# Keys and values of two heads in seven products instead of eight, and half of the gate-stage logits summed on ScalarE

## The chip, the cores and the metric

The kernel runs on one core of a Trainium2 chip. The metric is the device time of one execution in microseconds (us). TensorE (PE in the profile) multiplies matrices, VectorE (DVE) and ScalarE (ACT) work elementwise, GpSimd (POOL) and SyncE (SP) here mostly start transfers.

## What is computed

One decoder layer of a model with two branches side by side, for 528 prompt rows (16 of them meta tokens) and 32 sample rows (8 sequences of 4), so 560 rows in all, of width 2048.

```python
h = rmsnorm(x, g_pre)
q, k, v, ga, cb, cc, ch, gc, ma, mc = jnp.split(h @ w_in, split_offsets(), axis=-1)
a = attend(q, k, v, b_sb).reshape(bsz, t, D_ATTN) * jax.nn.silu(ga)
u = cc * ch
c = cb * causal_conv(u_ext, w_conv, b_conv) * jax.nn.silu(gc)
merged = (jax.nn.sigmoid(ma + b_gate[:D_MODEL]) * (a @ w_pa)
          + jax.nn.sigmoid(mc + b_gate[D_MODEL:]) * (c @ w_pc))
y = x + rmsnorm(merged @ w_out, g_post)
```

There are 8 heads of width 128. The prompt rows attend to one another; each sample row attends to 512 cached keys of its sequence, which lie in pages of 128, and to its own new rows. The logits of the sample rows against the cached keys (z = q·k for 8 sequences, 4 pages, 8 heads and 4 queries) are called decode logits below. Keys and values of all rows are outputs too.

## The kernel before

**Products.** All large products are float32 results made from halves: each operand is split into hi and lo (hi is the value cast to fp32r, lo what is left), and hi·hi, hi·lo and lo·hi are summed in PSUM. A weight block of 128 columns and 1024 rows comes as a tile `raw` over SP's queue (`w_load`), and `w_split` (L232 to L242) makes `whi` from it with a cast on ACT (L240) and `wlo` with a subtraction on DVE (L241). The normalized h lies transposed as `h_hi`, `h_lo`: 16 chunks of 128 rows of depth, each with 560 columns (one for each row of x).

**Heads.** `head_now` makes keys, values and the prompt attention of heads 0 to 3, `head_later` keys and values alone for heads 4 to 7. A projection (`k_proj`, `v_proj`) is a `gemm` with two ranges of 280 columns; each takes 16 chunks of depth by 3 products, so 96 matmuls (L256) a projection.

**Sums of h.** Behind the heads' projections, "tsum" (L935 to L966) prepares a Winograd form of Strassen's scheme: h is seen as 2 by 2 blocks, depth halves by column halves, of 274 columns. Three combinations of the blocks are made in float32 on DVE (the tiles r, x and y, in four pieces of 2 chunks), and split into `t_hi`, `t_lo` 0 to 2 by `t_split` (L943 the cast on ACT, L944 the subtraction on DVE). Then block (0,1) of h itself is overwritten in place with the combination r, `h_hi` and `h_lo` by the same two lines, also in four pieces. A piece of this can only be written when the last projection that needs the plain h has read it.

**Pairs.** From there on every projection is a pair: two neighbouring blocks of 128 columns of the weights (2 by 2 blocks with the depth halves) times h, in seven products instead of eight (`seven`, L986 on; `product`, L976 to L981, has 24 matmuls). In order these are: x from w11; q from s = w21 + w22; y, which starts as −x (a scaled copy on ACT, L1002), from s + w11 with t 0; x again, from w12; y from w21 + w11 with t 1; q again, from s + w12; y from w22 with t 2. Between them ACT copies q away as s5 (L1006) and y as s2 (L1009), and DVE makes c22 = y − s5 (L1015) and c12 = q − s2. The fifth product writes y and must wait for the copy s2, the seventh for c22. x and q lie in PSUM tiles named mm, of which there are three, y in the one named o. The gate stage takes 4 pairs of GA, then 16 pairs of the convolution in four groups of CC, CH, GC and CB, and later pairs of MA and MC.

**Decode logits.** `decode_steps` goes over units of a half of the heads and a sequence. A unit has four pages; a page of keys `kpage` comes over POOL's queue, and 16 instructions on DVE (L782, tile `junk`, 4 heads by 4 queries) multiply 128x128 elements with the query tile `qb` and sum along the row. Six units (DEC1) are done in the head stage ("part"), the rest in the gate stage ("logits"), at most a few pages behind a pair as `dec_group` counts them: `dec_step` moves the generator one page on. None of these is bound to a place.

**Order.** The kernel is written once, and a scheduler sets the order of each engine's instructions by its own model of the times. Instructions that `tc.keep_in_program_order` marks ("pin") stay in the order in which they are written. What the scheduler has set is final: each engine takes its instructions one after the other.

Of the kernel before, what the change touches and what calls it, by code (L numbers as in the profile page):

```python
# [17 lines left out]
P = 128  # L18
# [24 lines left out]
H = 8  # L43
# [4 lines left out]
DEC1 = 6  # L48
# [3 lines left out]
NOW = 4  # L52
LNEXP = "natural_log_exp_and_others"
# [7 lines left out]
def hybrid_step_kernel(  # L61
# [500 lines left out]
    def k_proj(h):  # L562
        o = proj(GATE_K + h * P, ALL)
        kr = hp.tile([P, T], F32, name="raw", bufs=2)
        for ob, s in nparts(o):
            act.copy(kr[:, s], ob)
# [6 lines left out]
        pe.matmul(zz, lhsT=kr[:, TP:T], rhs=qs_all[:, h, :], start=True, stop=True)  # L573
# [4 lines left out]
    def v_proj(h, pl=None):  # L578
        o = proj(GATE_V + h * P, ALL)
        vr = hp.tile([P, T], F32, name="raw", bufs=2)  # L580
        for ob, s in nparts(o):
            act.copy(vr[:, s], ob)
# [5 lines left out]
        if pl is None:  # L588
            pool.dma_start(vn_scr[h][0:512].rearrange("(a p) d -> p a d", p=P), vn[:, 0:4, :])
            pool.dma_start(vn_scr[h][512:TP], vn[0:16, 4, :])  # L590
            return None
        return v_split(pl, vn)
# [126 lines left out]
    def head_now(h):  # L719
# [5 lines left out]
        vhi, vlo = v_proj(h, np_)  # L725
# [4 lines left out]
        dec_step(2, "part")  # L730
# [4 lines left out]
    def head_later(h):  # L735
        pool.dma_start(k_scr[h], k_proj(h))
        dec_step(2, "part")
        v_proj(h)
        dec_step(2, "part")
# [20 lines left out]
    def decode_steps():  # L760
# [3 lines left out]
        for said, part in (("part", units[:DEC1]), ("logits", units[DEC1:])):  # L764
            with tc.tile_pool(name="dec1", bufs=2, side="right") as d1:
                for hf, b in part:
# [8 lines left out]
                    for pg in range(NPG):  # L775
                        kt = d1.tile([P, 512], F32, name="kpage", bufs=3)
                        first(page_load(kt, kc, b, pg, cs))
                        for i, qt in enumerate(qts):
                            for t in range(2):
                                for h in range(4):  # L780
                                    junk = d1.tile([P, P], F32, name="junk", bufs=2)
                                    dve.tensor_tensor_reduce(  # L782
                                        out=junk, in0=kt[:, h * P:(h + 1) * P], in1=qt[:, t, h * P:(h + 1) * P],
                                        scale=1.0, scalar=0.0, op0=ALU.mult, op1=ALU.add,
                                        accum_out=z_all[:, pg, b, 4 * hf + h, 2 * i + t:2 * i + t + 1])
                        yield
# [138 lines left out]
    for h in range(NOW, H):  # L925
# [7 lines left out]
    for i in range(3):  # L933
        ttp = tctx.enter_context(tc.tile_pool(name=f"tt{i}", bufs=1))
        t_hi.append(ttp.tile([P, 8, HU], F32R, name=f"t_hi{i}"))  # L935
        t_lo.append(ttp.tile([P, 8, HU], F32R, name=f"t_lo{i}"))
# [9 lines left out]
    with tc.tile_pool(name="tsum", bufs=2, side="right") as tsp:  # L946
        r1 = tsp.tile([P, 8, HU], F32, name="r1", bufs=1)
        for c in range(0, 8, 2):
# [3 lines left out]
            r, x, y = part(r1), *(tsp.tile([P, 2, HU], F32, name=n) for n in "xy")  # L952
# [33 lines left out]
    def seven(ws, n, rb, rt, s, tmp, sums=None):  # L986
# [14 lines left out]
        product(q, w_split(s), rb(0, 1), True, False)  # L1001
        act.activation(y, x, AF.Copy, scale=-1.0)  # L1002
        dve.tensor_add(s, s, w11)
        product(y, w_split(s), rt(0), False, False)
        s5 = tmp("s5")
        act.copy(s5, q)  # L1006
        product(x, w_split(w12), rb(1, 0), False, True)
        s2 = tmp("s2")
# [4 lines left out]
        product(y, w_split(w21), rt(1), False, False)  # L1013
        c22 = sums(1)
# [503 lines left out]
```

## Time and profile before

| | |
|---|---|
| time, median of 3 runs | 1578.59 us (1577.43 to 1579.0) |
| profiled execution, its own time | 1577.97 us |
| its span | 1576.4 us |
| DMA: bytes moved | 252.77 MB, mean 160 GB/s |
| heads, 100 to 366 us | PE busy 266.0 us |
| gates and convolution, 366 to 935 us | PE busy 566.83 us |

The stages follow one another in the span: the normalization and the first queries up to about 100 us, heads to 366, the pairs of GA and the convolution to about 935, the decode attention with the output of the heads, and the merge to the end. A row of the timeline gives start and length in us, then engine, line, operation, the tile written and the tiles read, and in brackets how long the engine was idle before it and what ended that. Line numbers are those of the kernel before.

### The profile page before, as it was taken

What the parts mean: (1) busy time and instruction counts of PE and PEld (TensorE: products, weight loads), DVE (VectorE), ACT (ScalarE), POOL (GpSimd) and SP (SyncE); (2) the same over time, 40 slices, a digit from 0 to 9 for tenths busy, and PEclk for the clock granted to TensorE, in tenths of its full rate; (3) what the DMA queues carried; (4) which work ended last, traced back from release to release, by engine and by line L of the source; (5) the groups of instructions that cost most, each with busy time, mean ns of one, the idle gap of its engine ahead of it and who ended that gap; (6) DMA issues with size and microseconds to landing.
All of it is one profiled execution on the core that took longest, in us unless ns stands there. A gap on an engine that the chain in (4) does not pass through costs nothing.

```text
span 1576.4 us, 32335 instructions
## 1 busy us (share of the span) xinstructions
PE 1557.6 (99%) x12172; PEld 1524.5 (97%) x12172; DVE 1262.8 (80%) x3574; ACT 753.0 (48%) x1339; POOL 235.5 (15%) x428
## 2 busy tenths in 40 slices
PE   8999999999999999999999999999999999999997
PEld 7999999999999999999999999898899999999997
DVE  7329999965799999999999996655678857877686
ACT  6245555435444444344444465444476733445562
POOL 1123333222111011001111103212100010000000
PEclk9999999999999999999999999999999999999999
DMA  8245556344564445445455547667595455443345
GB/s 264 82 139 178 170 160 187 112 125 131 161 183 137 142 133 162 145 124 170 118 166 174 162 130 236 191 190 229 157 310 181 129 186 171 147 117 86 102 139 188
DMA packets 300675, 252.77 MB, mean 160 GB/s; under 512 B 11522, under 2 KB 268614, under 8 KB 299702
## 3 DMA queue, kind: packets, MB, share of 16 engines
q1 hardware_dynamic: 272021, 160.45, 35.4%
q0 software_dynamic: 28368, 89.98, 17.1%
q8 instruction: 95, 1.56, 0.4%
q14 instruction: 63, 0.51, 0.1%
q10 hardware_dynamic: 128, 0.27, 0.1%
HBM read 217.95 MB, written 32.71 MB: 159 GB/s over the span
## 4 chain that ended last, share of the span: by engine, by line
PE 94%; DVE 4%; issue 1%; ACT 1%; DVEq 0%; ACTq 0%
PE mm L981 31%; PE mm L256 28%; PE o L981 24%; PE mm L321 2%; PE z L703 1%; PE o L715 1%; PE z L321 1%; PE tp L857 1%; DVE wlo L241 1%; PE z L621 1%; DVE junk L782 1%; PE z L1459 1%; PE tp L506 0%; PE z L1313 0%; DVE cv L1088 0%
## 5 line engine op out<-in xcount | busy, mean ns | idle before, releaser
L240 ACT CAST whi<-raw 128x1024 fp32r<-128x1024 f32 x247 | 259.2, 1051 | 338.3 <-PE mm L981 95.8
L241 DVE TENSOR_TENSOR wlo<-raw,whi 128x1024 fp32r<-128x1024 f32 x247 | 302.6, 1226 | 106.8 <-ACT whi L240 104.0
L981 PE MATMUL mm<-h_hi,whi 128*128 128x272 f32 (+1 forms) x1152 | 333.4, 290 | 0.2 <-ACT whi L240 0.2
L981 PE MATMUL mm<-h_lo,whi 128*128 128x272 f32 (+1 forms) x1152 | 333.3, 290 | 0.0
L981 PE MATMUL mm<-h_hi,wlo 128*128 128x272 f32 (+1 forms) x1152 | 331.2, 289 | 0.0
L981 PE MATMUL o<-t_hi,wlo 128*128 128x272 f32 (+1 forms) x864 | 249.7, 289 | 2.0 <-DVE wlo L241 2.0
L981 PE MATMUL o<-t_lo,whi 128*128 128x272 f32 (+1 forms) x864 | 249.8, 289 | 0.0
L981 PE MATMUL o<-t_hi,whi 128*128 128x272 f32 (+1 forms) x864 | 249.6, 289 | 0.0
L782 DVE CUSTOM_DVE_ANT_0 junk<-kpage,qb 128x128 f32<-128x128 f32 x1024 | 247.0, 292 | 2.8 <-DMA qb<-q_scr 2.3
L981 PEld LDWEIGHTS mm<-h_hi,whi 128*128 128x128 f32 x1152 | 217.4, 189 | 6.3 <-ACT whi L240 3.7
L981 PEld LDWEIGHTS mm<-h_lo,whi 128*128 128x128 f32 x1152 | 216.8, 188 | 1.5 <-issue 1.2
L981 PEld LDWEIGHTS mm<-h_hi,wlo 128*128 128x128 f32 x1152 | 216.6, 189 | 0.1
L241 DVE TENSOR_TENSOR wlo<-s,whi 128x1024 fp32r<-128x1024 f32 x126 | 155.0, 1230 | 59.8 <-ACT whi L240 59.6
L240 ACT CAST whi<-s 128x1024 fp32r<-128x1024 f32 x126 | 132.1, 1048 | 145.6 <-PE mm L981 50.3
L256 PE MATMUL mm<-h_lo,whi 128*128 128x280 f32 (+1 forms) x640 | 187.6, 293 | 0.0
L256 PE MATMUL mm<-h_hi,wlo 128*128 128x280 f32 (+1 forms) x640 | 187.1, 293 | 0.0
L256 PE MATMUL mm<-h_hi,whi 128*128 128x280 f32 (+1 forms) x640 | 186.7, 292 | 0.0
L981 PEld LDWEIGHTS o<-t_hi,wlo 128*128 128x128 f32 x864 | 163.1, 189 | 3.0 <-DVE wlo L241 3.0
L981 PEld LDWEIGHTS o<-t_lo,whi 128*128 128x128 f32 x864 | 163.4, 189 | 0.0
L981 PEld LDWEIGHTS o<-t_hi,whi 128*128 128x128 f32 x864 | 162.9, 189 | 0.0
L256 PEld LDWEIGHTS mm<-h_lo,whi 128*128 128x128 f32 x640 | 120.3, 188 | 0.8
L256 PEld LDWEIGHTS mm<-h_hi,wlo 128*128 128x128 f32 x640 | 120.5, 188 | 0.5
(448 smaller groups left out, 3167.7 us busy)
## 6 DMA issues: line engine op xcount, KB each, us to landing
raw<-in_w_in SPq DMA_DIRECT2D x192, 512.0 KB, 4.5
kpage<-in_cache_k POOLq DMA_DIRECT2D x64, 256.0 KB, 3.7
qb<-q_scr POOLq DMA_DIRECT2D x32, 512.0 KB, 5.8
vpage<-in_cache_v POOLq DMA_DIRECT2D x64, 256.0 KB, 6.0
raw<-in_w_out SPq DMA_DIRECT2D x32, 512.0 KB, 4.1
gate_scr<-g POOLq DMA_DIRECT2D x32, 272.0 KB, 3.0
gt<-gate_scr POOLq DMA_DIRECT2D x16, 544.0 KB, 4.6
raw<-in_w_pc SPq DMA_DIRECT2D x16, 512.0 KB, 5.0
```

The costliest lines, as they stand in the source:

```text
L240: act.copy(hi, x)
L241: dve.tensor_sub(lo, x, hi.bitcast(F32))
L256: pe.matmul(o, lhsT=w, rhs=r[:, t0:t1], start=(k == 0 and n == 0), stop=(k == nk - 1 and n == 2))
L321: pin(pe.matmul(o, lhsT=l, rhs=r[:, k, t0:t1], start=(start and m == 0), stop=(stop and m == 2), skip_group_check=True))
L621: pe.matmul(zt[:m, c0:c0 + n], lhsT=l[:, s0:s0 + m], rhs=r[:, ts:ts + n], start=(c0 == 0 and i == 0), stop=(i == 2), skip_group_check=True)
L703: pe.matmul(o, lhsT=l, rhs=x, start=False, stop=(i == len(ops) - 1), skip_group_check=True)
L715: pe.matmul(ot[:, ts - NMETA:ts - NMETA + n], lhsT=l[:m, st, :], rhs=x[:m, c0:c0 + n], start=False, stop=(g == GROUPS[-1] and i == 2), ski ...
L782: dve.tensor_tensor_reduce(out=junk, in0=kt[:, h * P:(h + 1) * P], in1=qt[:, t, h * P:(h + 1) * P], scale=1.0, scalar=0.0, op0=ALU.mult, o ...
L857: pin(pe.matmul(po[32 * j:32 * (j + 1), :], lhsT=lhs, rhs=rhs, start=(pg == 0), stop=last and n >= len(vts) - 4, tile_position=(0, 32 * j) ...
L981: pe.matmul(o, lhsT=l[:, k, :], rhs=r, start=(start and k == 0 and m == 0), stop=(stop and k == 7 and m == 2), skip_group_check=True)
L1459: pin(pe.matmul(o, lhsT=(m1, m2)[h][:, k + 8 * (q == 1), ts], rhs=two[h][q == 2][:, :, k, :], start=(n == 0), stop=(n == 47)))
```

## The change

Two things are changed together.

First, only heads 4 and 5 stay in `head_later`. Keys of heads 6 and 7 are one pair, their values another (`later_pair`), in seven products with 280 columns. They stand right behind tsum and ahead of the first pair of GA. For them the blocks of h and the t tensors are 280 columns wide instead of 274. What was in `k_proj` and `v_proj` is cut into `raw_of`, `k_out`, `v_out`, `k_store` and `v_store`, which both ways call.

Second, five units of logits instead of six are done in the head stage, with the plain instructions. In the gate stage queries 0 and 1 go as before, and for queries 2 and 3 DVE multiplies a whole page with the query row (`kq`, 128x512), and ACT sums each head's 128 columns with an accumulating copy. A step is now one query of a page instead of a page; `seven` calls `dec_tick` behind each product, from the V pair's end on and up to the count of 27, and these multiplications on DVE are pinned.

```diff
-DEC1 = 6
+DEC1 = 5
+SOLO = 6
...
     def head_later(h):
-        pool.dma_start(k_scr[h], k_proj(h))
+        k_store(h, k_proj(h))
         dec_step(2, "part")
-        v_proj(h)
-        dec_step(2, "part")
+        v_store(h, v_proj(h))
+
+    def later_pair(c, h, qs=None):
+
+        raws = [hp2.tile([P, T], F32, name="raw", bufs=2) for _ in range(2)]
+        seen = []
+        for m, half, b in pair(c + h * P, HC):
+            act.copy(raws[m][:, NMETA + half * HQ:NMETA + (half + 1) * HQ], b[:, HM:])
+            act.copy(raws[m][:, half * HM:(half + 1) * HM], b[:, :HM])
+            seen.append(m)
+            if seen.count(m) < 2:
+                continue
+            if qs is not None:
+                k_store(h + m, raws[m])
+                k_out(hp2, h + m, raws[m], qs[:, m, :])
+            else:
+                v_store(h + m, v_out(hp2, h + m, raws[m]))
+        dec_group()
...
-                        for i, qt in enumerate(qts):
-                            for t in range(2):
...
+                        for t in range(DT):
+                            if t < 2:
+                                direct(t, pin)
+                            else:
+                                kq = d1.tile([P, 512], F32, name="kq", bufs=2)
+                                pin(dve.tensor_mul(kq, kt, qts[1][:, t % 2, :]))
                                 for h in range(4):
...
+                                    x = kq[:, h * P:(h + 1) * P]
+                                    act.activation(x, x, AF.Copy, accum_out=z_at(h, t))
+                            yield
...
-        if n <= 25:
-            dec_step((0, 2, 2, 2)[n - 1] if n <= 4 else 1 if n <= 20 else 4, "logits")
-        else:
-            dec_step(2 if n in (26, 28) else 1)
+        if n == 1:
+            dec_step(1, "logits")
+        elif n == 27:
+            dec_step(64, "logits")
+        elif n > 27:
+            dec_step(2 if n in (28, 30) else 1)
+
+    def dec_tick():
+
+        if 1 <= n_group[0] < 27:
+            dec_step(1, "logits")
...
-    for h in range(NOW, H):
+    for h in range(NOW, SOLO):
         head_later(h)
...
     def blk(x, i, j):
-        return x[:, 8 * i:8 * i + 8, (j + 1) * HC - HU:(j + 1) * HC]
+        return x[:, 8 * i:8 * i + 8, j * HC:(j + 1) * HC]
...
         product(x, w_split(w11), rb(0, 0), True, False)
+        tick()
...
+    with tc.tile_pool(name="heads2", bufs=1) as hp2:
+        qs = hp2.tile([P, H - SOLO, TS], F32, name="qs")
+        for h in range(SOLO, H):
+            pool.dma_start(qs[:, h - SOLO, :], qt_scr[h][:, PQ:TQ])
+        later_pair(GATE_K, SOLO, qs)
+        later_pair(GATE_V, SOLO)
...
-                after = hl[0].tile([P, P], F32, name="after")
-                dve.tensor_scalar_add(after, neg_u.bitcast(F32), 1.0)
...
+    after = hs0.tile([P, P], F32, name="after")
+    dve.tensor_scalar_add(after, neg_u.bitcast(F32), 1.0)
```

Beside these, `head_now` ends with a step of one page instead of two. In the order, PE has 12,026 instructions with matrices instead of 12,074, and DVE 64 `junk` instructions fewer ahead of the sums of h.

What stands on DVE where the first pair begins, in the kernel before: the last small copies of the last head (L511, L512), then the four pieces of the in-place block, mixed with the first pair's weights.

```order
L241 TENSOR_TENSOR wlo<-raw,whi 128x1024 x2
L511 COPY nat<-tp 16x128
L512 COPY ks<-tp 32x128
L944 TENSOR_TENSOR h_lo<-r_5282,h_hi 128x2x274 x3
L241 TENSOR_TENSOR wlo<-s,whi 128x1024
L944 TENSOR_TENSOR h_lo<-r_5282,h_hi 128x2x274
L1003 TENSOR_TENSOR s<-s,raw 128x1024
L241 TENSOR_TENSOR wlo<-s,whi 128x1024
```

All rows that make t_lo lie further ahead. In the changed kernel the same place, where the first pair is that of K, reads as follows; L994 is now the line of `t_split`, L242 that of wlo, L1012 and L1013 the sums for t 2, and t 0, 1 and 2 are named 4554, 4559 and 4564 (their hi halves one less).

```order
L994 TENSOR_TENSOR h_lo<-r_4568,h_hi 128x2x280
L994 TENSOR_TENSOR t_lo_4554<-x,t_hi_4553 128x560
L994 TENSOR_TENSOR t_lo_4559<-y,t_hi_4558 128x560
L1012 TENSOR_TENSOR x<-h_hi,x 128x560
L994 TENSOR_TENSOR t_lo_4554<-x,t_hi_4553 128x560
L994 TENSOR_TENSOR t_lo_4559<-y,t_hi_4558 128x560
L1013 TENSOR_TENSOR x<-x,h_lo 128x560
L994 TENSOR_TENSOR h_lo<-r_4568,h_hi 128x2x280 x2
L1012 TENSOR_TENSOR x<-h_hi,x 128x560
L242 TENSOR_TENSOR wlo<-s,whi 128x1024
L994 TENSOR_TENSOR h_lo<-r_4568,h_hi 128x2x280
```

The first piece of the in-place block has moved ahead of every piece of t_lo. Thirty more rows follow before c22, among them y's wlo and the other pieces of t_lo.

On ACT, in the second half of the K pair of the changed kernel (L993 is the cast of `t_split`, L241 that of whi, and the tile s_4787 is s2):

```order
L993 CAST t_hi_4553<-x 128x560 x2
L993 CAST t_hi_4558<-y 128x560
L241 CAST whi<-s 128x1024
L993 CAST t_hi_4563<-x 128x560
L241 CAST whi<-raw 128x1024
L1063 COPY s_4787<-o 128x280
L993 CAST t_hi_4558<-y 128x560
L993 CAST t_hi_4563<-x 128x560
```

The copy of y out of PSUM, for which PE's fifth product waits, stands behind casts for t and for weights of later products, where before only weight casts stood there.

More of the change, by code (lines that the diff above doesn't have):

```diff
@@ L560, in v_split, with raw_of, k_out @@
         return vhi, vlo
-    def k_proj(h):
-        o = proj(GATE_K + h * P, ALL)
-        kr = hp.tile([P, T], F32, name="raw", bufs=2)
+    def raw_of(o):
+        raw = hp.tile([P, T], F32, name="raw", bufs=2)
         for ob, s in nparts(o):
-            act.copy(kr[:, s], ob)
+            act.copy(raw[:, s], ob)
+        return raw
+    def k_out(hp, h, kr, qs):
         kn = hp.tile([P, 5, P], F32, name="nat", bufs=2)
@@ L572, in k_proj, with v_out @@
         zz = z_ps()[0:TS, 0:TS]
-        pe.matmul(zz, lhsT=kr[:, TP:T], rhs=qs_all[:, h, :], start=True, stop=True)
+        pe.matmul(zz, lhsT=kr[:, TP:T], rhs=qs, start=True, stop=True)
         act.activation(z_new[:, :, h, :], zz.rearrange("p (b t) -> p b t", t=DT), AF.Identity,
                        bias=bsb[0:TS, h:h + 1])
-        return kr
[L578 to L582, printed above, removed]
+    def k_proj(h):
+        kr = raw_of(proj(GATE_K + h * P, ALL))
+        k_out(hp, h, kr, qs_all[:, h, :])
+        return kr
+    def v_out(hp, h, vr):
         vn = hp.tile([P, 5, P], F32, name="nat", bufs=2)
@@ L729, in head_now @@
         ot = next(attend(np_, h, khi, klo, vhi, vlo, *q_split(np_, qr)))
-        dec_step(2, "part")
+        dec_step(1, "part")
         at = np_.tile([P, PQ], F32, name="at", bufs=1)
@@ L777, in decode_steps, with z_at, direct @@
                         first(page_load(kt, kc, b, pg, cs))
-                        for i, qt in enumerate(qts):
-                            for t in range(2):
-                                for h in range(4):
[L781 to L786, printed above, removed]
+                        def z_at(h, t):
+                            return z_all[:, pg, b, 4 * hf + h, t:t + 1]
+                        def direct(t, pin=lambda ins: ins):
+                            for h in range(4):
+                                junk = d1.tile([P, P], F32, name="junk", bufs=2)
+                                pin(dve.tensor_tensor_reduce(
+                                    out=junk, in0=kt[:, h * P:(h + 1) * P], in1=qts[t // 2][:, t % 2, h * P:(h + 1) * P],
+                                    scale=1.0, scalar=0.0, op0=ALU.mult, op1=ALU.add, accum_out=z_at(h, t)))
+                        if said == "part":
+                            for t in range(DT):
+                                direct(t)
+                            yield
+                            continue
+                        if pg == 0 and (hf, b) == part[0]:
+                            yield
+                        for t in range(DT):
+                            if t < 2:
[3 more added lines that the diff above has]
+                                pin(dve.tensor_mul(kq, kt, qts[1][:, t % 2, :]))
+                                for h in range(4):
+                                    x = kq[:, h * P:(h + 1) * P]
+                                    act.activation(x, x, AF.Copy, accum_out=z_at(h, t))
+                            yield
             yield said
@@ L950, in part @@
                 return (blk(x, *ij) if ij else x)[:, c:c + 2]
-            r, x, y = part(r1), *(tsp.tile([P, 2, HU], F32, name=n) for n in "xy")
+            r, x, y = part(r1), *(tsp.tile([P, 2, HC], F32, name=n) for n in "xy")
             dve.tensor_sub(r, part(h_f, 0, 0), part(h_f, 0, 1))
@@ L984, in hybrid_step_kernel, with seven @@
     block_22 = [None]
-    def seven(ws, n, rb, rt, s, tmp, sums=None):
+    def seven(ws, n, rb, rt, s, tmp, sums=None, tick=lambda: None):
         def behind(ins):
@@ L1037, in rt @@
         def rt(i):
-            return lambda k: (t_hi[i][:, k, HU - n:HU], t_lo[i][:, k, HU - n:HU])
+            return lambda k: (t_hi[i][:, k, HC - n:], t_lo[i][:, k, HC - n:])
         ws = blocks_of(win, c)
         s = sp2.tile([P, 8, P], F32, name="s")
-        yield from seven(ws, n, rb, rt, s, lambda name: sp2.tile([P, HU], F32, name=name)[:, :n])
+        yield from seven(ws, n, rb, rt, s, lambda name: sp2.tile([P, HC], F32, name=name)[:, :n], tick=dec_tick)
     gctx, uctx = ExitStack(), ExitStack()
     sp2 = gctx.enter_context(tc.tile_pool(name="sums", bufs=1))
+    with tc.tile_pool(name="heads2", bufs=1) as hp2:
[4 more added lines that the diff above has]
+        later_pair(GATE_V, SOLO)
     gp = gctx.enter_context(tc.tile_pool(name="gates", bufs=2))
```

28 lines of the change are left out of this document (18 added, 10 removed).

## The prediction, made before the changed kernel was run

> **What bounds the kernel now.** I began with the page: busy shares, then the chain that ended last.
>
> ```profile
> span 1576.4 us, 32335 instructions
> ...
> PE 1557.6 (99%) x12172; PEld 1524.5 (97%) x12172; DVE 1262.8 (80%) x3574; ACT 753.0 (48%) x1339; POOL 235.5 (15%) x428
> ...
> PE 94%; DVE 4%; issue 1%; ACT 1%; DVEq 0%; ACTq 0%
> ```
>
> TensorE (PE) is idle for 1576.4 − 1557.6 = 18.8 us of the span, and the chain lies on it for 94%. A matmul less is time less, and a wait that PE did not have is time more; DVE and ACT count only where PE waits for them. So next I read what PE waits for, and then the busy time by stage (span of the window, then PE, PEld, DVE, ACT, POOL with counts, clock, DMA share, GB/s).
>
> ```profile
> PE o L981 <- DVE wlo L241: 2.0, 4, 0.5
> PE mm L981 <- ACT whi L240: 0.7, 2, 0.5
> ...
> 316.00:366.00 50.00, 50.00 (x393) 49.38 (x392) 28.17 (x41) 19.16 (x38) 11.93 (x20) 1.00 0.37 110
> 366.00:935.00 569.00, 566.83 (x4482) 565.45 (x4481) 533.45 (x1759) 258.24 (x387) 66.15 (x112) 1.00 0.51 153
> ```
>
> Between 316 and 366 us, where heads 6 and 7 make keys and values, PE is busy for the whole 50.00 us and DVE for 28.17. In the gate stage (366 to 935) PE loses 2.2 us, and DVE is busy for 533.45 of 569: it is nearly full. The change puts DVE-hungry seven-product work in the place where DVE has room, and shifts DVE's logits.
>
> **What the change removes: 48 matmuls.** The step of a matmul comes from the chain of waits (start, length, what); the group means of the page, 290 ns, are latencies that overlap.
>
> ```profile
> 347.18 9.13 PE mm L256 x71
> 356.31 0.44 PE tp L506 x4
> ...
> 360.42 5.26 PE mm L256 x41
> 365.68 3.03 PE mm L981 x24
> ```
>
> 5.26/41 = 0.1283 and 9.13/71 = 0.1286 us: 0.1284 for 280 columns. Two heads with keys and values are 4 × 96 = 384 such matmuls; two pairs are 2 × 7 × 24 = 336. **−48 × 0.1284 = −6.2 us.** PE is full there, so all of it counts, if the pairs run as densely.
>
> **What it moves: the sums of h meet the first pair.** Before, the t tensors were complete long before the first pair.
>
> ```profile
> 332.15 0.73 DVE L944 TENSOR_TENSOR t_lo<-x,t_hi 128x548 fp32r<-128x548 f32 x1 [0.87 <-ACT t_hi L943]
> ...
> 360.11 0.65 ACT L943 CAST h_hi<-r 128x548 fp32r<-128x548 f32 x1 [0.27 <-PE mm L256]
> ...
> 360.46 0.28 DVE L511 COPY nat<-tp 16x128 f32<-16x128 f32 x1 [5.90 <-PE tp L510]
> 360.67 0.27 DVE L512 COPY ks<-tp 32x128 f32<-32x128 f32 x1
> 360.86 0.71 DVE L944 TENSOR_TENSOR h_lo<-r,h_hi 128x548 fp32r<-128x548 f32 x1
> ```
>
> The last t_lo ended at 332.9, and the first pair's product began at 365.68, 33 us later. Call the start of the first pair S. Its block of h is overwritten in place, and a piece waits for the matmuls of the last plain projection that read it: the first h_hi cast began at S − 5.57 and its h_lo at S − 4.82. In the changed order the first pair is K of heads 6 and 7, right behind V of head 5, and that same in-place h_lo (first row of the DVE rows shown with the change) stands **ahead of** all t_lo pieces. DVE executes its rows in order: it sat 5.90 us at the nat copy until PE delivered. So no t_lo begins before about S − 4.1, however early DVE gets there, and what was spread over 50 us comes at once.
>
> [...]
>
> Steps of DVE, start to start:
>
> ```profile
> 290.58 2.66 DVE L953 TENSOR_TENSOR r<-h_hi 128x548 f32<-128x548 f32 x4
> 293.15 1.37 DVE L954 TENSOR_TENSOR r<-r,h_lo 128x548 f32<-128x548 f32 x2
> ...
> 328.80 1.21 DVE L241 TENSOR_TENSOR wlo<-raw,whi 128x1024 fp32r<-128x1024 f32 x1
> 329.93 0.71 DVE L963 TENSOR_TENSOR x<-x,h_lo 128x548 f32<-128x548 f32 x1
> ```
>
> (293.15 − 290.58)/4 = 0.64 for 548 columns, so 0.655 for 560; 329.93 − 328.80 = 1.13 for 1024, taken as 1.14. With these I walk the DVE rows from S − 4.8:
>
> - up to y's wlo (L242 from s, the second one behind the in-place piece): 16 rows of 560 columns (10.5), three of 1024 (3.4), two small copies (0.4): 14.3 us, so S + 9.5. The first t_hi also waits for head 3's attention store to land, since the tile's memory is that of the heads: the store takes 3.0 us (row below) and is issued some 7 us ahead of S in the new order, so t_hi ends near S − 3.5 and all shifts by 0.6: **S + 10.1**. PE has x and q behind it at 48 × 0.1284 and some transposes, 6.9. The third product starts 3.2 us late.
> - to the last piece of t_lo0: 8 rows of 560, three of 1024: 8.7 more, **S + 18.7**. y's product ends at 19.4, where without waits it would be at 10.
> - to the copy s2 of y, which the fifth product waits for. On ACT it stands behind two weight casts (0.96 each, 362.51 to 363.47 in the rows below) and a t_hi cast that were issued ahead of it: about **S + 21.3**.
> - to c22, which the seventh product waits for: 8 rows of 560, two of 1024, one of 280 (0.35): 7.9 behind 18.7, so 26.6 at least, 27.8 with the late copy. The seventh product then runs for 24 × 0.1284 = 3.1: the pair ends at **S + 29.7 to 30.9**.
>
> ```profile
> a_scr<-at POOLq DMA_DIRECT2D x4, 256.0 KB, 3.0
> ...
> 362.51 1.05 ACT L240 CAST whi<-s 128x1024 fp32r<-128x1024 f32 x1
> 363.47 0.64 ACT L943 CAST h_hi<-r 128x548 fp32r<-128x548 f32 x1
> ```
>
> PE's work in that time is 168 × 0.1284 plus transposes of V5 (0.44 and 0.22 in two places) = 22.6 us. **The K pair waits 7.1 to 8.3; I take 8.** It is unseen as yet. It can't be below nothing, because PE idles nowhere in 316 to 366. Low end: DVE delivers everything but y's wlo in time, 3.2. High end: each DVE row takes its whole duration (0.72 and 1.21 in the rows above) instead of its step, which makes some 33 us of 31, and ACT's late rows slip by as much again: 12. The V pair behind it finds t ready, and takes DVE only 11 weight rows of 1.14, twelve and a half of 21.6 us: no wait. The first GA pair is as before.
>
> **What it moves: the logits.** One unit of 64 products (64 × 0.21 = 13 us of DVE) leaves the head stage, where PE did not wait: nothing gained. In the gates half of the products become 88 multiplications of 512 columns and 352 accumulating copies on ACT.
>
> ```profile
> L782 DVE CUSTOM_DVE_ANT_0 junk<-kpage,qb 128x128 f32<-128x128 f32 x640 | 155.5, 293 | 2.3 <-DMA qb<-q_scr 2.3
> ...
> 289.82 0.30 DVE L782 CUSTOM_DVE_ANT_0 junk<-kpage,qb 128x128 f32<-128x128 f32 x1
> 290.03 0.09 DVE L782 DVE_READ_ACCUMULATOR2_ANT z_all<- 128x1 f32 x1
> 290.03 0.30 DVE L782 CUSTOM_DVE_ANT_0 junk<-kpage,qb 128x128 f32<-128x128 f32 x1
> ...
> 1400.74 0.27 ACT L1306 ACTIVATE sq<-z 128x128 f32<-128x128 f32 x1
> 1400.91 0.19 ACT L1306 ACTIVATION_READ_ACCUMULATOR sq<-z 128x1 f32 x1
> 1401.13 0.28 ACT L1306 ACTIVATE sq<-z 128x128 f32<-128x128 f32 x1
> ```
>
> DVE in the gates: 640 × 0.21 = 134 us before; 352 × 0.21 + 88 × 0.60 (0.64 × 512/548) = 127 after. ACT gains 352 × 0.39 = 137 us on 258 of 569: 69%, behind no wall, though each group of four puts 1.6 us ahead of a weight cast. What counts is the spread. Before, an ordinary conv pair carried one page (16 × 0.21 = 3.4 us); after, seven ticks of 0.84 or 0.60, 5.0. With the pair's other rows the pair of GC, which has the convolution's rows as well, goes from 22.8 to 24.3 us of DVE against 168 × 0.126 = 21.2 of PE (3.03/24 above, 272 columns). It was late already:
>
> ```profile
> 500.09 1.23 DVE L241 TENSOR_TENSOR wlo<-s,whi 128x1024 fp32r<-128x1024 f32 x1
> 501.23 1.08 DVE L1091 SCALAR_TENSOR_TENSOR cv<-u,wcv,cv 128x512 f32<-128x512 f32 x3
> ```
>
> This wlo, behind the convolution, is where the four waits of 0.5 (first waits row) fall. In the new order it stands in the same place behind the same rows: those 2.0 stay. The surplus of 1.5 goes into the CB pair, whose third wlo comes some 0.5 late: **+1.9 in four groups**. Bounds: −2.7 (both waits rows vanish, as pins now spread the logits evenly) and +6 (all of 1.5 is waited for, four times). I stay near the row, 0.5. The first logits' wait for qb, 2.3 on DVE, now falls where DVE has little lead: +0.3, between 0 and 2.3. The loads: weights are 4 MB as before and the DMA share is 0.37 in that window; the qs load (two of 16 KB) stands on POOL's queue ahead of the pairs and is used 25 us later; the stores of K and V land long before their readers near 1160. I price these at nothing, and at most at one landing, 3 us, if a raw buffer is held by a late store. `after` moves to a later tile: one small row.
>
> **Sum**, from the profiled execution's own 1577.97: −6.2 + 8 + 1.9 + 0.3 = +4.0, 1582.0. That execution lies 0.6 under the median of 1578.59, so **1582.5**.
>
> **Rivals.** *K pair waits, gates don't* : the pins take logits out of the way of wlo everywhere; −6.2 + 8 + 0.3 − 2.7 = −0.6, about 1578. For it: five pairs that had 13.4 us of logits (four pages) now have 5.0. Against: the four waits lie in pairs that had one page, and get more. *The clock*: a long idle stretch is followed by a low clock in this trace:
>
> ```profile
> 10.00:15.00 5.00, 3.65 (x16) 3.28 (x16) 3.95 (x9) 4.94 (x9) 0.00 (x0) 0.50 1.03 266
> ```
>
> The granted clock is 0.50 there, after thin work. The K pair's third product is starved in pieces between S + 7 and S + 19; if that halves the clock for some 6.5 us, as long as it lasted near 10 us, PE loses 3.2 more: 1585.7. [...] *Only the matmuls count* (the other side: faster): DVE keeps ahead of PE in the K pair because the pieces arrive in the order in which PE eats them, k by k, and only wlo's 3.2 is waited for, partly hidden by w12's product which needs no t; −6.2 + 1.5 to 3.2, with the gates between −2.7 and 0: 1570.5 to 1575.6, about 1573. It decides if y's wlo ends before S + 9 and t_lo0 before S + 12, which needs half of the rows counted above to be gone. *ACT in the way of whi*: the four accumulations ahead of a cast delay one product by 0.5 in most of 26 pairs, up to 13 us: 1590. That the change doesn't do what it says is out: the 48 matmuls are missing in the order.
>
> **How the numbers follow.** Forecast (1579.5 to 1586): 0.48. K pair waits, gates don't (1575 to 1580): 0.25. Only the matmuls (1570.5 to 1575.6): 0.12. Clock (1584 to 1589): 0.10. ACT (1586 up): 0.05. A measurement of this kernel can tell about 0.2%, 3.2 us, from no change: 1575.4 to 1581.8. Under it lies the third rival and a little of the first, 0.16; within it most of the first and two fifths of the forecast, 0.40; over it the rest, 0.44. The range 1574.0 to 1588.0 leaves out most of the third rival and part of the last.
>
> **What would show it.** In the waits of PE: rows of its o product for t_lo and wlo, 5 us or more in all, within 30 us of S near 314; the K pair's 168 matmuls lasting 30 us from first to last, the V pair's 21.6; TensorE's count 48 lower; the clock at 1.00 in these windows. In the gates: DVE's wlo rows again at the head of PE's waits, eight instead of four. If PE's idle time near S is under 3 us, the walk along DVE's rows is wrong, and the time falls to about 1573; if it is over 12, ACT's order or the landing of the store was mis-sized.

## The result, and the profile after

| | median | runs |
|---|---|---|
| before | 1578.12 us | 6, from 1577.43 to 1581.58 |
| changed | 1589.49 us | 6, from 1588.27 to 1592.89 |

The ratio is 1.0073, with a 95% interval of 1.0059 to 1.0087: the changed kernel is slower by 11.4 us. The forecast was slower by 4, and 1589.49 lies above the range given (to 1588). The profiled execution of the changed kernel took 1592.89.

The same rows of the page as before, of the changed kernel:

```profile
span 1591.3 us, 32339 instructions
...
PE 1563.1 (98%) x12124; PEld 1524.9 (96%) x12124; DVE 1257.3 (79%) x2976; ACT 864.2 (54%) x2055; POOL 240.4 (15%) x430
...
PE 88%; DVE 8%; issue 2%; ACT 2%; DVEq 0%; POOL 0%; ACTq 0%; POOLq 0%
```

There are 48 matmuls fewer, as said, but PE is idle for 28.2 us instead of 18.8, and it is busy for 5.5 us more: a matmul at a lower clock counts as busy (22 at a clock of 0.50 are busy for 5.21 us, in the K pair below). What PE waits for, over the span (us in total, times, longest):

```profile
PE mm L1031 <- ACT whi L241: 4.2, 8, 1.2
PE z L712 <- ACT hi L496: 2.1, 1, 2.1
...
PE o L1031 <- DVE wlo L242: 1.9, 4, 0.6
PE o L1031 <- ACT s L1063: 1.7, 1, 1.7
...
PE tp L1160 <- ACT lt L1158: 1.1, 1, 1.1
```

Most of PE's rows are the same in both kernels and in the same order, so the start of a given matmul in one trace can be set against its start in the other. The shift, after minus before:

| stretch, in time of before | what is there | shift at its end | change |
|---|---|---|---|
| 0 to 23 us | start, the same instructions | +3.7 | +3.7 |
| 23 to 269 | heads, the same instructions | +3.6 | −0.1 |
| 269 to 369 | heads' end, sums of h, the two pairs | +10.8 | +7.2 |
| 369 to 830 | GA, convolution, first merge pair | +14.9 | +4.1 |
| 830 to the end | the rest | +14.5 | −0.4 |

The first line is not the change: it is 3.7 us over instructions that are equal in both, and over all the executions profiled for this study it came out between 0 and 3.8, whatever the kernel. It goes with the speed of the first matmuls: in the changed kernel's execution those of 256 columns step in 0.21 to 0.22 us up to 24.2 us and in 0.11 to 0.12 us behind that, and the first 24 of L177 take 5.38 us. In that of before the same 24 (L176) take 2.98 us, and the granted clock is 0.50 from 9.53 to 16.36 us. The shift is taken off everywhere below. What is left, 10.8, agrees with the medians. The matmuls gave −6.2 (48 × 0.1284), so the second part of the heads lost 13.3 and the gates, up to the end, lost 3.7.

**Head 3, 2.1 us of the 13.3.** This is the wait of `z` for `hi` in the list above. ACT's row and the one of GpSimd (POOL) that it waited for, in the changed kernel's timeline:

```profile
277.65 0.54 ACT L496 CAST hi<-r 128x416 fp32r<-128x416 f32 x1 [4.70 <-POOL r L642]
...
271.27 6.35 POOL L642 TENSOR_SCALAR_AFFINE_SELECT r<-r 128x128 f32<-128x128 f32 x2 [5.29 <-DVE r L477]
...
273.50 1.38 DVE L1004 TENSOR_TENSOR r<-r,h_lo 128x560 f32<-128x560 f32 x2
274.80 0.73 DVE L1005 TENSOR_TENSOR r<-r,h_lo 128x560 f32<-128x560 f32 x1
275.45 1.21 DVE L242 TENSOR_TENSOR wlo<-raw,whi 128x1024 fp32r<-128x1024 f32 x1
276.59 0.73 DVE L1005 TENSOR_TENSOR r<-r,h_lo 128x560 f32<-128x560 f32 x1
```

Two selects (the causal mask of head 3's attention) took 6.35 us, the first of them 6.2. They ended at 277.6, just as VectorE's gapless run of sums for r ended (276.59 + 0.73 = 277.3). The same two selects in the kernel before, and the VectorE rows beside them:

```profile
265.44 1.56 POOL L633 TENSOR_SCALAR_AFFINE_SELECT r<-r 128x128 f32<-128x128 f32 x2 [2.32 <-DVE r L476]
...
265.22 0.28 DVE L782 CUSTOM_DVE_ANT_0 junk<-kpage,qb 128x128 f32<-128x128 f32 x1
265.43 0.28 DVE L782 CUSTOM_DVE_ANT_0 junk<-kpage,qb 128x128 f32<-128x128 f32 x1
265.66 1.28 DVE L241 TENSOR_TENSOR wlo<-raw,whi 128x1024 fp32r<-128x1024 f32 x1
```

The unit of 64 products that the change takes out of the head stage had stood there; without it the sums of h move up beside the attention. Those products read two tiles as well, but in short rows of 0.28 us; even then the second of the two selects (1.17 us) ended with a long row, that of wlo (266.9), while the next two, at 271.55 us beside products alone, took 0.58. By what the long rows hold a select up no run shows.

**The K pair, 11.2 us.** Windows of the changed kernel (span of the window, then PE, PEld, DVE, ACT, POOL, clock, DMA share, GB/s), and rows at the points of the prediction's walk:

```profile
319.00:338.25 19.25, 15.14 (x104) 13.31 (x102) 19.25 (x27) 9.07 (x16) 3.59 (x6) 1.00 0.42 112
338.25:345.07 6.82, 5.21 (x22) 5.21 (x23) 6.10 (x9) 2.77 (x5) 0.00 (x0) 0.50 0.14 39
345.07:352.20 7.13, 6.72 (x52) 6.49 (x51) 4.25 (x6) 3.39 (x8) 2.72 (x5) 1.00 0.51 151
...
334.84:338.25 3.41, 1.71 (x9) 1.17 (x8) 3.41 (x6) 2.41 (x4) 0.00 (x0) 1.00 0.72 197
...
312.31 0.28 DVE L512 COPY nat<-tp 16x128 f32<-16x128 f32 x1 [5.69 <-PE tp L511]
...
314.30 0.74 DVE L994 TENSOR_TENSOR h_lo<-r,h_hi 128x560 fp32r<-128x560 f32 x1 [1.52 <-ACT h_hi L993]
314.96 0.73 DVE L994 TENSOR_TENSOR t_lo<-x,t_hi 128x560 fp32r<-128x560 f32 x1
...
327.40 1.21 DVE L242 TENSOR_TENSOR wlo<-s,whi 128x1024 fp32r<-128x1024 f32 x1
...
336.50 0.72 DVE L994 TENSOR_TENSOR t_lo<-x,t_hi 128x560 fp32r<-128x560 f32 x1
...
339.42 0.38 ACT L1063 COPY s<-o 128x280 f32<-128x280 f32 x1
...
340.73 0.43 PE L1031 MATMUL o<-t_hi,whi 128*128 128x280 f32 x1
340.96 0.43 PE L1031 MATMUL o<-t_lo,whi 128*128 128x280 f32 x1
```

The pair's first product began at S = 318.8. From 319 to 338.25 us VectorE is busy for the whole 19.25 us and PE for 15.14. Then, for 6.82 us, the granted clock is 0.50. PE goes on at 339.86, when `s` is copied, and a matmul steps in 0.23 us (340.73 to 340.96) instead of 0.128: 22 matmuls take 5.2 us instead of 2.8. That is 2.4 us more. No single wait of PE ahead of the drop was longer than 1.2 us (the longest of the pair, 1.7 for `s` in the list above, began only as the clock fell). But in the last 3.41 us ahead of it (fourth row) PE was busy for half of the time, 1.71 us.

**The gates, 3.7 us.** Three of the four waits for wlo in the pairs of GC are still there (the fourth in the list above is the K pair's). In the first GC pair PE waits for a transpose instead (`lt`, 1.1). New are a wait of 0.3 for whi in each CB pair of the other three groups, and two of 0.4 in the first merge pair. On ACT and DVE, ahead of the CB wait at 620 us and of the first merge pair:

```profile
618.00 1.05 ACT L241 CAST whi<-s 128x1024 fp32r<-128x1024 f32 x1 [0.51 <-DVE s L1055]
...
806.21 1.23 DVE L1051 TENSOR_TENSOR s<-raw 128x1024 f32<-128x1024 f32 x1 [2.17 <-DMA raw<-in_w_in]
```

In the CB pair the cast waits for VectorE's sum s, not behind ScalarE's sums. Ahead of the merge pair VectorE itself waits 2.17 us until a weight block has landed. Experiments 7 and 10 to 12 are on the gates.

### The profile page after: what moved, and what is told of

It reads as the page before. It is cut to its first block, busy times and chain, and to the rows that moved or that the text cites. A ratio compares the mean times of both kernels' runs of the same rounds, so it can differ in the third digit from the quotient of the medians.

```text
span 1591.3 us, 32339 instructions
## 1 busy us (share of the span) xinstructions
PE 1563.1 (98%) x12124; PEld 1524.9 (96%) x12124; DVE 1257.3 (79%) x2976; ACT 864.2 (54%) x2055; POOL 240.4 (15%) x430
## 4 chain that ended last, share of the span: by engine, by line
PE 88%; DVE 8%; issue 2%; ACT 2%; DVEq 0%; POOL 0%; ACTq 0%; POOLq 0%
PE mm L1031 30%; PE o L1031 23%; PE mm L257 23%; PE mm L322 2%; DVE wlo L242 2%; PE z L712 1%; PE o L724 1%; PE z L322 1%; ACT whi L241 1%; PE tp L900 1%; DVE junk L809 1%; PE z L630 1%; PE z L1522 1%; DVE cv L1154 1%; DVE kq L825 0%
## 5 line engine op out<-in xcount | busy, mean ns | idle before, releaser
L241 ACT CAST whi<-raw 128x1024 fp32r<-128x1024 f32 x247 | 258.6, 1050 | 290.3 <-PE mm L1031 88.1
L242 DVE TENSOR_TENSOR wlo<-raw,whi 128x1024 fp32r<-128x1024 f32 x247 | 302.7, 1226 | 99.1 <-ACT whi L241 96.2
L1031 PE MATMUL mm<-h_hi,whi 128*128 128x272 f32 (+2 forms) x1216 | 353.4, 291 | 3.7 <-ACT whi L241 3.6
L1031 PE MATMUL mm<-h_lo,whi 128*128 128x272 f32 (+2 forms) x1216 | 351.3, 289 | 0.0
L1031 PE MATMUL mm<-h_hi,wlo 128*128 128x272 f32 (+2 forms) x1216 | 350.5, 290 | 0.1
L1031 PE MATMUL o<-t_hi,whi 128*128 128x272 f32 (+2 forms) x912 | 265.5, 291 | 3.0 <-ACT s L1063 1.7
L1031 PE MATMUL o<-t_hi,wlo 128*128 128x272 f32 (+2 forms) x912 | 265.2, 291 | 1.9 <-DVE wlo L242 1.9
L1031 PE MATMUL o<-t_lo,whi 128*128 128x272 f32 (+2 forms) x912 | 264.4, 290 | 0.5 <-DVE t_lo L994 0.5
L1031 PEld LDWEIGHTS mm<-h_hi,whi 128*128 128x128 f32 x1216 | 229.7, 189 | 12.3 <-ACT whi L241 8.8
L1031 PEld LDWEIGHTS mm<-h_hi,wlo 128*128 128x128 f32 x1216 | 228.9, 189 | 0.5 <-DVE wlo L242 0.3
L1031 PEld LDWEIGHTS mm<-h_lo,whi 128*128 128x128 f32 x1216 | 229.1, 188 | 0.1
L242 DVE TENSOR_TENSOR wlo<-s,whi 128x1024 fp32r<-128x1024 f32 x132 | 161.6, 1224 | 79.8 <-ACT whi L241 79.8
L241 ACT CAST whi<-s 128x1024 fp32r<-128x1024 f32 x132 | 138.3, 1048 | 102.3 <-PE mm L1031 42.0
L828 ACT ACTIVATE kq<-kq 128x128 f32<-128x128 f32 x352 | 104.5, 299 | 30.4 <-DVE kq L825 30.0
L257 PE MATMUL mm<-c_hl,whi 128*128 128x272 f32 x512 | 100.3, 288 | 0.0
```

Source lines behind the costliest of these rows:

```text
L241: act.copy(hi, x)
L242: dve.tensor_sub(lo, x, hi.bitcast(F32))
L257: pe.matmul(o, lhsT=w, rhs=r[:, t0:t1], start=(k == 0 and n == 0), stop=(k == nk - 1 and n == 2))
L828: act.activation(x, x, AF.Copy, accum_out=z_at(h, t))
L1031: pe.matmul(o, lhsT=l[:, k, :], rhs=r, start=(start and k == 0 and m == 0), stop=(stop and k == 7 and m == 2), skip_group_check=True)
```

## The experiments

Each was run with the kernel before on the same chip; all medians stand in this table, and the columns on the right come from the shifts in the traces, without the start. The first is from 269 us to the first pair of GA, less −6.2 where two pairs replace plain heads (−3.1 for one): the loss there. The second is the gates up to the end.

| | median | ratio to before, 95% | heads' end and pairs | gates to the end |
|---|---|---|---|---|
| changed | 1589.49 | 1.0059 to 1.0087 | +13.3 | +3.7 |
| 1 logits alone | 1588.92 | 1.0048 to 1.0072 | +2.3 | +7.4 |
| 2 pairs alone | 1583.27 | 1.0016 to 1.0033 | +12.0 | −1.4 |
| 3 six units | 1587.91 | 1.0043 to 1.0067 | +12.2 | +2.2 |
| 4 t first | 1592.70 | 1.0068 to 1.0094 | +14.7 | +3.4 |
| 5 one pair, V | 1575.46 | 0.9970 to 0.9989 | +0.1 | −0.8 |
| 6 t of 280 columns | 1577.48 | 0.9983 to 1.0001 | 0.0 | −1.3 |
| 7 no ScalarE sums | 1584.77 | 1.0026 to 1.0053 | +14.0 | −1.5 |
| 8 other operation for r | 1590.43 | 1.0061 to 1.0092 | +13.6 | +2.7 |
| 9 no lo sums | 1574.13 | 0.9957 to 0.9982 | +2.3 | −1.4 |
| 10 no pins | 1614.76 | 1.0205 to 1.0243 | +13.4 | +26.5 |
| 11 one copy | 1590.24 | 1.0056 to 1.0089 | +12.3 | +4.1 |
| 12 three buffers | 1590.04 | 1.0051 to 1.0085 | +13.3 | +2.7 |

**1 and 2: the two halves of the change, each alone.** In 1, heads 6 and 7 stay plain:

```diff
-SOLO = 6
+SOLO = 8
...
-        later_pair(GATE_K, SOLO, qs)
-        later_pair(GATE_V, SOLO)
+    dec_group()
+    dec_group()
```

> The change of the logits alone: heads 6 and 7 plain as before, five units in the head stage, ticks and ScalarE sums in the gates. Theory A (the changed kernel's trace split by its own shifts: matmuls -6.2, head 3's attention +2.3, K pair +10.7, gates +4.0): the gates cost +4.0 on their own and the shorter head stage hides head 3 or costs 2, so 1582 to 1584. Rival B (all of the loss comes from the two pairs, the gates only show it): 1578, as before.

In 2, the logits are those of before, in the head stage and in the gates:

```diff
-DEC1 = 5
+DEC1 = 6
...
-        if n == 1:
-            dec_step(1, "logits")
-        elif n == 27:
-            dec_step(64, "logits")
-        elif n > 27:
-            dec_step(2 if n in (28, 30) else 1)
+        if n <= 25:
+            dec_step((0, 2, 2, 2)[n - 1] if n <= 4 else 1 if n <= 20 else 4, "logits")
+        else:
+            dec_step(2 if n in (26, 28) else 1)
...
-        if 1 <= n_group[0] < 27:
-            dec_step(1, "logits")
+        return
```

> The two pairs alone: six units in the head stage and the logits of before in the gates. Theory A: -6.2 for the matmuls, the K pair's wait with its clock of about +10.7, no late attention of head 3 as the 64 products again stand between the sums of h on VectorE, gates as before: 1582.5, K pair about 33 us long. Rival B (the logits' change is what costs): 1572 to 1574. Rival C: the wait of the K pair comes from head 3's late attention, which frees the memory of the t tensors; then it shrinks here too, to 3 to 6, and the time is 1575 to 1578.

Both halves lose: 1588.92 and 1583.27. Theory A is met for the pairs alone (1582.5 forecast) and its cause too: head 3's attention is early again there (its store is issued at 297.4, against 311.7 in the changed kernel), yet the pair waits as long, so rival C falls. The logits alone missed both expectations, by 5. Of their 9.7, 2.3 are the select at head 3, as expected, and 4.7 are lost between 382 and 407 us: without the V pair ahead, the first query and key tiles land 7.9 us after issue, the pinned products wait for them, and ScalarE's sums of these pages then stand in front of two weight casts. PE waits 1.8 and 0.4 us, and the clock is 0.50 for 3.4 us behind that. The last 2.7 are the rest of the gates.

**3: six units in the head stage again.**

```diff
-DEC1 = 5
+DEC1 = 6
...
-        dec_step(1, "part")
+        dec_step(2, "part")
```

> The changed kernel with six units of logits in the head stage again instead of five. Theory A: GpSimd's select of head 3 is slow because VectorE runs the sums of h without a gap; with 64 products between them it takes under 1 us again and PE does not wait at it: 2.3 less than the changed kernel, 1587. In the gates 160 ticks instead of 176, up to 1 less. Rival C: with head 3's attention earlier, the K pair shrinks as well: 1580 to 1584. Rival D (the select waits for something else): 1589.5.

GpSimd's rows in this kernel:

```profile
265.55 1.56 POOL L642 TENSOR_SCALAR_AFFINE_SELECT r<-r 128x128 f32<-128x128 f32 x2 [2.32 <-DVE r L477]
271.66 0.58 POOL L642 TENSOR_SCALAR_AFFINE_SELECT r<-r 128x128 f32<-128x128 f32 x2 [1.40 <-DVE r L477]
```

With the 64 products back, the selects are as fast as before and the wait at head 3 is gone. That much of Theory A holds. The median fell by 1.6 (the traces by 2.6: 2.1 at head 3 and 1.5 in the gates), because the K pair lost 12.2 instead of 11.2: the sums of h begin later by those products.

**4: the in-place block behind t.**

```diff
-            t_split(part(t_hi[2]), part(t_lo[2]), x)
+            t_end = t_split(part(t_hi[2]), part(t_lo[2]), x)
...
-            t_split(blk(h_hi, 0, 1)[:, c:c + 2], blk(h_lo, 0, 1)[:, c:c + 2], r1[:, c:c + 2])
+            with tc.issue_after(t_end.ins):
+                t_split(blk(h_hi, 0, 1)[:, c:c + 2], blk(h_lo, 0, 1)[:, c:c + 2], r1[:, c:c + 2])
```

> The changed kernel with the in-place block of h behind the last piece of t on VectorE. By the prediction's step (the in-place piece blocks the t_lo rows behind it) t_lo starts some us earlier and the K pair's wait falls by 3 or more: 1586 or less. Rival C (t waits for its memory until head 3's attention is stored, and VectorE's whole work of 30 us is what counts): q, which reads that block, becomes what is late, and the time is the same or up to 5 worse: 1589 to 1595.

1592.70, no better, as the rival in the expectation had it. The first t_lo waits for its own t_hi instead:

```profile
311.95 0.74 DVE L994 TENSOR_TENSOR t_lo<-x,t_hi 128x560 fp32r<-128x560 f32 x1 [2.07 <-ACT t_hi L993]
```

Here S is 315.90, so t_lo begins at S − 3.95, against S − 3.85 in the changed kernel: moving the in-place piece alone frees nothing. That its place is not what sets the loss, experiment 3 shows: there VectorE has no idle time above 0.1 us from 294 us on, through S at 312.96, and the pair still loses 12.2. It is the amount of VectorE work that is not done when the pair begins.

**5: values of heads 6 and 7 as a pair, their keys plain, logits as before.**

```diff
-    for h in range(NOW, SOLO):
+    for h in range(NOW, H):
         head_later(h)
...
-            v_store(h, v_proj(h))
+            if h < SOLO:
+                v_store(h, v_proj(h))
...
-        later_pair(GATE_K, SOLO, qs)
         later_pair(GATE_V, SOLO)
```

> Keys of heads 6 and 7 plain, their values as one pair, six units in the head stage and the logits of before in the gates. Theory A (the pair pays when VectorE has the time of two more projections, 24.6 us, for the sums of h): no wait in the first pair, the clock stays at 1.00, 24 matmuls less (-3.1), and the drift of the gates seen in the pairs-only run (-1.4, t tensors 280 wide): 1574 to 1575. Rival (any first pair of 280 columns behind the heads waits for t): 1578 to 1586.

1575.46 is faster than before, by 0.21% (0.11 to 0.30). The window of its only new pair, and VectorE's last piece of t:

```profile
340.40:363.00 22.60, 22.60 (x178) 22.34 (x178) 14.83 (x17) 10.52 (x20) 4.05 (x7) 1.00 0.51 155
...
338.31 0.72 DVE L978 TENSOR_TENSOR t_lo<-x,t_hi 128x560 fp32r<-128x560 f32 x1
```

PE is busy for all of the 22.60 us, at clock 1.00. t was complete at 339.0, only 1.4 us ahead of S (340.4): two plain projections more, 24.6 us of PE, are just what VectorE needed.

**6: t of 280 columns in the kernel before.** The same in all tiles of tsum, and the tile `after` moves as in the change.

```diff
-        return x[:, 8 * i:8 * i + 8, (j + 1) * HC - HU:(j + 1) * HC]
+        return x[:, 8 * i:8 * i + 8, j * HC:(j + 1) * HC]
...
-            return lambda k: (t_hi[i][:, k, HU - n:HU], t_lo[i][:, k, HU - n:HU])
+            return lambda k: (t_hi[i][:, k, HC - n:], t_lo[i][:, k, HC - n:])
```

> The kernel before with nothing but t tensors and in-place block 280 columns wide (and the small tile that makes room for them moved, as in the change). If the slow drift of the gates in the pairs-only run, -1.4 between 369 and 1182 us, comes from where the columns of t start, it stands here too: 1577. If it comes from something else: 1578.6.

Its trace ends 1.29 us earlier than that of before, with the same instructions, in small steps over the pairs: the mean step from an `o` matmul of 272 columns to the next matmul goes from 126.1 to 125.4 ns (380 to 930 us), most of it behind `o<-t_lo` (126.6 to 124.8). In the medians this is 0.08%, and the interval touches no change. It is a gain that the prediction didn't have.

**7: all queries as products on VectorE, at the same ticks.**

```diff
-                            if t < 2:
+                            if t < DT:
```

> The changed kernel with all four queries of a page as VectorE's products, at the same ticks: nothing summed on ScalarE. Theory A (the gates' loss is VectorE's load in the pairs of GC and CB, ScalarE's sums are not in the way): VectorE has 0.24 us more on every second tick, some 0.9 a pair, and the gates' loss grows: 1592 to 1598. Rival (the sums on ScalarE stand in front of weight casts and cost most of the 4): 1586 to 1588.

1584.77, 4.7 less than the changed kernel, though VectorE's logits take longer (0.84 instead of 0.60 on every second tick). Theory A is wrong by sign. In the gates only the waits of before are left (the list of PE's waits from 380 to 935 us has this row alone):

```profile
PE o L1031 <- DVE wlo L242: 2.2, 4, 0.5
```

**8: another operation for r.** In the changed kernel:

```diff
-            dve.tensor_sub(r, part(h_f, 0, 0), part(h_f, 0, 1))
-            dve.tensor_add(r, r, part(l_f, 0, 0))
-            dve.tensor_sub(r, r, part(l_f, 0, 1))
+            for a, b, op in ((part(h_f, 0, 0), part(h_f, 0, 1), ALU.subtract), (r, part(l_f, 0, 0), ALU.add),
+                             (r, part(l_f, 0, 1), ALU.subtract)):
+                dve.scalar_tensor_tensor(out=r, in0=a, scalar=1.0, in1=b, op0=ALU.mult, op1=op)
```

> The changed kernel with the twelve sums that make r written as SCALAR_TENSOR_TENSOR (times 1.0, then the same sum) in nearly the same order. If the operation TENSOR_TENSOR is what keeps GpSimd's select waiting (6.35 us for two), the select takes about 1 us again beside the twelve and PE's 2.1 at head 3 goes: 1587. If any gapless run of VectorE does it: as the changed kernel, 1589.5.

The two selects take 6.35 us again and PE waits 2.1: beside SCALAR_TENSOR_TENSOR rows they are as long as beside TENSOR_TENSOR.

**9: pairs alone, with less VectorE work for t.** The five sums of each piece that add the lo halves of h are left out.

```diff
-            dve.tensor_add(r, r, part(l_f, 0, 0))
-            dve.tensor_sub(r, r, part(l_f, 0, 1))
...
-            dve.tensor_add(x, x, part(l_f, 1, 1))
...
-            dve.tensor_add(y, y, part(l_f, 0, 0))
...
-            dve.tensor_add(x, x, part(l_f, 1, 0))
```

> The pairs-only kernel (six units, logits of before) without the lo halves of h in the sums: 20 of the 48 rows of VectorE for t and r are left out, 13 us; everything else stands. Theory A (the K pair waits for VectorE's 30 us of rows, the clock drop follows from that wait): the pair's excess of 12 shrinks to 0 to 3 and the clock in it stays at or near 1.00: 1573 to 1576. Rival (the place of the in-place block, or the pair itself, is what waits): 1580 or more.

1574.13, and the loss at the pair falls from 12.0 to 2.3. The first 25 us of the pair in experiment 2 and here:

```profile
319.00:344.00 25.00, 18.20 (x110) 16.18 (x108) 24.23 (x35) 11.12 (x16) 3.59 (x6) 0.86 0.32 87
```

```profile
316.50:341.50 25.00, 23.34 (x181) 22.81 (x180) 21.80 (x26) 12.35 (x25) 6.86 (x12) 1.00 0.47 142
```

13 us less of VectorE rows take 9.7 from the loss, and the clock, 0.86 over the stretch in experiment 2, is 1.00 here. The wait is VectorE's, and the clock follows from the wait.

**10 to 12: what costs in the gates.** 10 leaves out the pins on VectorE's logits:

```diff
-                                direct(t, pin)
+                                direct(t)
...
-                                pin(dve.tensor_mul(kq, kt, qts[1][:, t % 2, :]))
+                                dve.tensor_mul(kq, kt, qts[1][:, t % 2, :])
```

11 replaces the four sums by one copy of four columns, so the sums of queries 2 and 3 are left out:

```diff
-                                for h in range(4):
-                                    x = kq[:, h * P:(h + 1) * P]
-                                    act.activation(x, x, AF.Copy, accum_out=z_at(h, t))
+                                act.copy(z_all[:, pg, b, 4 * hf:4 * hf + 4, t], kq.rearrange("p (h d) -> p h d", d=P)[:, :, 0])
```

and 12 gives kq a third buffer:

```diff
-                                kq = d1.tile([P, 512], F32, name="kq", bufs=2)
+                                kq = d1.tile([P, 512], F32, name="kq", bufs=3)
```

> The changed kernel without the pins on VectorE's logits in the gates; products and ScalarE's sums as in the change. Theory A (the sums on ScalarE and the rows they need cost the 5 in the gates, wherever the logits stand): 1588 to 1590. Rival (the pinned places cost it): 1584 to 1585.

> The changed kernel with VectorE's multiplications kept and the four accumulating copies of each replaced by one copy of four columns: the sums over the 128 columns of queries 2 and 3 are left out. If ScalarE's time (352 sums, 103 us in steps of 0.293) is what costs the 5 in the gates, they go: 1584 to 1585. If the multiplications on VectorE and their places are what costs: 1588 to 1590.

> The changed kernel with three buffers for the products kq instead of two. If VectorE's pinned multiplication waits until ScalarE has summed the one before the last, and rows behind it wait with it, a third buffer takes most of that away: 1586 to 1588. If ScalarE's occupation or VectorE's load is the cause: 1589 to 1590.

Without pins the kernel takes 1614.76: neither expectation, and the reverse of the rival. The scheduler then puts the logits where the gates lose 26.5. There the sums on ScalarE do stand in the way: in GA's pairs eight of them in a row run ahead of the casts that PE waits for (1.05 and 0.43 us), and twice in the gates the clock falls to 0.50 for 3.4 us. With ScalarE's sums gone (11) nothing is gained, though ACT's part of the logits is now this row, 17 us instead of 104.5 for the sums and 66.3 for the reads of the accumulator (which overlap them):

```profile
L826 ACT COPY z_all<-kq 128x4 f32<-128x4 f32 x88 | 17.3, 198 | 41.2 <-DVE kq L825 41.0
```

The third buffer doesn't help either. So neither ScalarE's time nor the wait for its buffer is what the gates of the changed kernel lose. What differs between 7 and 11 can be counted in the traces: the logits' rows that VectorE begins in each pair, as 0.21 us for a product and 0.60 for a kq, and the pair's length, from the first of its 168 matmuls to the first of the next 168:

| second to fourth conv group | pair of GC: logits, length | pair of CB: logits, length |
|---|---|---|
| before | 3.4, 22.1 to 22.2 us | 5.3, 21.1 |
| changed | 4.5, 22.2 | 5.6 to 5.8, 21.9 |
| 7, products only | 3.4, 22.1 | 5.5, 21.1 |
| 11, one copy | 4.9, 22.6 | 4.7 to 5.3, 21.7 to 21.8 |

Where products and kq alternate, the scheduler puts 1.0 to 1.7 us more of them into these two pairs, which are those where VectorE also has the convolution, and fewer into the pairs of CC and CH (9.9 us together instead of 12.4), where there is room. In GC's and CB's pairs together the loss is 0.8 for the changed kernel.

## Why the prediction was wrong

**The saving** was right: 48 matmuls, −6.2.

**The K pair's walk** was right in its numbers and half right in its reason. y's wlo ended at S + 9.8 (10.1 forecast), the last piece of t_lo0 at S + 18.4 (18.7), the copy s2 at S + 21.0 (21.3). VectorE's rows do set the pair. The reason given for them coming late, that they are blocked up to S − 4, is there in the changed kernel: VectorE stood idle for 5.69 us at the nat copy and 1.52 at the in-place piece, and the first t_lo began at S − 3.85. But the blocking is not what decides: in experiment 3 there was none and the loss was 12.2. (Experiment 4, with the in-place piece moved behind, gained nothing, but there t_lo waited for t_hi, so it doesn't settle this.) Experiments 5 and 9 show it: either 24.6 us more of projections or 13 us less of rows takes the loss away, nearly or wholly. Without the clock the changed kernel's pair lost 8.8, where 8 was taken.

**The clock** failed as a case of its own. It stood among the rivals with a chance of 0.10 and 3.2 us, tied to a long idle stretch. None ahead of the drop was above 1.2 us, and the clock dropped all the same: +2.4. What the forecast left out is what such waits come to together: of the 3.41 us ahead of the drop, 1.71 were busy. Nor does the row that the forecast quotes stand behind an idle stretch: from 6.12 to 9.53 us of the trace of before PE was busy for the whole 3.41 us (small matmuls, 16x128), and from there to 16.36 us the clock was 0.50. That trace has an idle stretch ahead of a low clock at its end alone: no matmul from 1566.00 to 1569.42 us, and 0.50 from there.

The clock dropped in the first pair of every kernel in which that pair lost 10 us or more (the changed one, 2 to 4, 7, 8 and 10 to 12), down to 0.50 to 0.74 as the mean of windows of 5 to 7 us, and stayed at 1.00 in the pairs of 5 and 9. So it belonged into the forecast as a term that follows from the wait.

**The step that failed most plainly** is "One unit of 64 products leaves the head stage, where PE did not wait: nothing gained." It was costed at nothing, with no look at what moves up in its place. What moved up, the sums of h, ran without a gap beside head 3's selects on GpSimd and made them 6.35 us long: +2.1 at PE. Experiments 3 and 1 show it from both sides: with 64 products there it goes, without them it comes, with or without pairs.

**The gates** were a mis-sized term: +2.2 forecast (1.9 and 0.3), 3.7 measured. The mechanism was the one named, VectorE's surplus in GC's pair that falls on CB's: 0.8 in each of four groups, where 0.5 was taken (it reaches PE through VectorE's sum s and whi, not through wlo). What was not foreseen is +1.4 in the first merge pair and a gain of 1.3 over the pairs, as t is 280 columns wide. The 1.4 go with a weight block that lands late: VectorE's idle time ahead of that pair is 2.17 us in the changed kernel and 2.23, 1.24, 2.59 and 1.53 in experiments 4, 8, 11 and 12, where the pair loses 1.2, 0.5, 1.6 and 0.8; in 3 and 7 there is no such idle time, and no loss. That ScalarE's sums would stand in the way of whi, the last rival, fell with experiment 11 for the changed kernel; in experiments 1 and 10 they do stand there.

Together: 2.1 for head 3, 2.4 for the clock, 0.8 for the pair, 1.5 for the gates; 6.8 on a forecast of 4.0 make 10.8, as in the traces. Why the weight block of the first merge pair lands late, and by which of its estimates the scheduler spreads two kinds of logits worse than one, stays open.

## What to carry to other kernels

Work that is brought forward needs its operands earlier: count the helper engine's rows that must end before it, from where they can begin, and not only their order. When a filler leaves an engine, ask what takes its place and who runs beside that. And where a wait of PE is forecast in pieces of a microsecond, add them up and price a slower clock with them: in the changed kernel PE was busy for 1.71 of the 3.41 us ahead of the drop, no wait there was above 1.2, and the clock cost 2.4. Here half of such a change, the pair that had the time, was faster than either kernel (1575.46).

## What was not expected of the hardware

A select of GpSimd on 128x128 elements, 0.28 and 0.34 us beside VectorE's short products in the kernel before (head 3, from 271.55 us on), took 6.2 in the changed kernel beside gapless TENSOR_TENSOR rows with two inputs; with SCALAR_TENSOR_TENSOR rows there (experiment 8) two selects took the same 6.35 together. The clock fell to 0.50 for 6.8 us without any wait of PE above 1.2 us ahead of it. All changes of the granted clock in one trace lie a multiple of 3.41 us apart (at 24.22, 338.25, 345.07 and 1584.11 us in the changed kernel's, at 9.53, 16.36 and 1569.42 in that of before). In the changed kernel's first pair it fell behind such a stretch of 3.41 us with PE busy for 0.50 of it, and not behind the three ahead of that, with 0.65, 0.79 and 0.86. That is no sharp limit: at head 3 a stretch with 0.58 (276.81 to 280.22 us) kept the full clock, and in the trace of before the clock fell at 9.53 us behind one with 1.00. The same matmuls stepped by 0.7 ns less on average when the t tensors were 280 columns wide instead of 274 (126.1 to 125.4 ns, experiment 6). And 352 accumulating copies on ScalarE, 0.29 us apart (the prediction took 0.39), cost PE nothing that could be seen in the changed kernel: 1589.49 us with them, 1590.24 with one copy in the place of four (experiment 11).
